# When the next weight unit is fetched in the attention layer, and where its subtraction stands in VectorE's order

## The chip, the cores and the metric

The kernel runs on one core of a Trainium2 chip. The metric is device time in microseconds (us) of one execution, as the median of several runs. A core has engines with instruction queues of their own: TensorE (PE, with its weight loads shown apart as PEld), VectorE (DVE), ScalarE (ACT), GpSimd (POOL) and SyncE (SP), which here only issues DMAs. Each engine works through its list in order; an instruction that has to wait holds what stands behind it in the same list.

## The reference

A trunk of four residual blocks on x of shape (1, 512, 1024) in float32: softmax attention, an MLP, a gated linear recurrence (RG-LRU), and again an MLP, with an RMSNorm ahead of each and one at the end. The change touches the attention alone:

```
qkv = einsum('bsd,de->bse', h, w_qkv).reshape(B, S, 3, 16, 64)
s = einsum('bqhd,bkhd->bhqk', q_c, k_band) * 64**-0.5 + bias    # relative bias, own chunk of 64 and 8 before
p = softmax(where(key_pos >= 0, s, -1e30))
o = einsum('bhqk,bkhd->bqhd', p, v_band);  out = o @ w_o        # out is added to the residual
```

## The kernel before

**Products.** A float32 product is made of three matmuls (`mm3`, lines 288 to 290): each operand is split into a rounded high part and the rest as a low part, and high by high, low by high and high by low are summed in one PSUM bank.

**Weight units.** The weights come as a list of units (`plan`), each a 128x1024 float32 tile of 512 KB. `fetch` (from line 140) takes the next unit: a DMA that SP issues (line 154) into one of three raw tiles `wr`, a cast on ACT that gives the high part `wh` (line 179), and a subtraction on DVE that gives the low part `wl` (line 184). `wh` and `wl` rotate through five buffers each. `prefetch(n)` fetches until n units are ready and not yet taken; `want(n)` prefetches n + `ahead` units and takes n. In the attention, `ahead` is 4, so a projection that begins on unit u fetches unit u+4 at its first line. In what follows wl18 is the subtraction of unit 18, and so on. Units 10 to 15 are the q and k projections of the head pairs 2 to 4 (q on the even number), 16 to 19 together the second half of the v projection (v1), 20 to 25 q and k of the pairs 5 to 7, 26 to 33 the output projection (wo), and then the MLP's.

**Attention.** 16 heads. For head h, `score` makes the scores on PE in three PSUM banks (lines 483 and 484); DVE adds the bias and takes the maximum while it reads them (line 487, tile `p`), negates it (491), ACT takes the exponential with a running sum (494), DVE makes the reciprocal (498) and scales (501, four instructions). `turn` transposes p on PE (line 514, ten matmuls into three banks `x`), ACT casts it (`pH`, 518) and DVE subtracts (`pL`, 519). `weigh` multiplies by v (529 and 530), and ACT and DVE bring the halves of a pair together (`ax` 535, `o` 536, `oH` 540, `oL` 541). Scores and transposes share one pool of four PSUM banks, taken in turn; projections have another four.

**Projections between the heads.** The projections of later pairs are a queue of small steps (`queue`, `fill`) put between the parts of the heads: q and k of a pair (`qk_steps`: 24 matmuls into one bank, then `q_out` or `k_out`), v (`v_steps`), and the output projection (`wo_steps`). `q_out` scales (tile `tq`, line 384), casts and subtracts (389). `k_out` scales (`tk`, line 394), casts each half on ACT (`kh`, 399), subtracts on DVE (`kl`, 400) and copies both to the other 64 partitions by 128 KB DMAs on SP (lines 401 and 402).

**Order.** The program is written in this order; a scheduler then sets the order on each engine by the order of the program and by its own estimate of when inputs are there, and may move instructions past each other. `tc.keep_in_program_order(ins)` keeps one instruction at its place in the program's order.

Of the kernel before, what the change touches and what calls it, by code (L numbers as in the profile page):

```python
# [35 lines left out]
def f(ap):  # L36
    return ap.bitcast(F32)
# [3 lines left out]
def trunk(ctx: ExitStack, tc: tile.TileContext, xT, cols, gfin, win, wqkv, wo, rwin, rga, rgx, rwo, w1, w2, out):  # L41
# [10 lines left out]
    def mmp(name):  # L52
        return ps.tile([P, T], F32, name=name, tag="mm")
# [46 lines left out]
    state = {"next": 0, "ready": [], "ahead": 4, "stop": None, "plain": 0}  # L100
    raws, start_, down, upper = {}, [], {}, {}

    def two(t):
        return t.rearrange("p (k c) -> p k c", k=2)
# [4 lines left out]
    def rows(src):  # L109
        return src.rearrange("(k p) c -> p k c", p=P)  # L110

    def load_down(key, name):
        if key not in down:
            return
        both = state["raw"].tile([P, 2, 1024], F32, name=f"b{name}_{key[0]}{key[1]}", tag=f"b{name}")
        for h in range(2):
            raws[name, h] = both[:, h]
            nc.sync.dma_start(two(raws[name, h]), rows(down[key][name][h * U : (h + 1) * U]))

    def first_sum(key):  # L120
        if key in down:
            for h in range(2):
                G.dma_start(raws["12", h], raws["11", h], accum_op=ALU.add)

    def load_up(key, name):
        if key not in upper:
            return
        if name in ("s1", "22"):
            raw = state["kept"][:, int(name == "22")]
        else:  # L130
            n = state["base"] + int(name == "12")
            raw = wraw.tile([P, 1024], F32, name=f"u{name}_{key[0]}{key[1]}", tag=f"wr{n % 3}")
        raws["u" + name] = raw
        nc.sync.dma_start(four(raw), rows(upper[key]["21" if name == "s1" else name]))
        if name == "s1":
            G.dma_start(four(raw), rows(upper[key]["22"]), accum_op=ALU.add)

    def fetch():
        i = state["next"]
# [4 lines left out]
        n, half = 1024, nk  # L144
        if kind[:5] == "plain":
            n = nk * sum(src.shape[1] for src in key)
# [37 lines left out]
        low = V.tensor_sub(L[:, :n], raw[:, :n], f(H[:, :n]))  # L184
        if not i:
            start_.append(low)
        if kind == "plain_":
            state["base"] = state["plain"] % 3
            load_up((nk_layer[i], 0), "11")
            load_up((nk_layer[i], 0), "12")  # L190
        elif kind == "us2" and key[1]:
            load_up(following, "s1")
        elif kind == "us3":
            load_up(following, "11")
        elif kind == "us4":
            load_up(following, "12")
        elif kind == "u22" and key[1]:
            load_up(following, "22")
        elif kind in ("11", "t1", "22", "21", "t2", "t3", "t4") and key[1] == 3:
            hs = slice(half * U, (half + 1) * U)  # L200
            if kind == "t1":
                nc.sync.dma_start(two(raws["11", half]), rows(down[key]["22"][hs]))
                G.dma_start(two(raws["11", half]), rows(down[key]["12"][hs]), accum_op=ALU.add)
            elif kind == "22":
                G.dma_start(raws["22", half], raws["12", half], accum_op=ALU.add)
        elif kind == "t2" and half:
            load_down(following, "12")
        elif kind == "t3" and half:
            load_down(following, "11")
        elif kind == "t4" and half:  # L210
            first_sum(following)
            load_down(following, "22")
            load_down(following, "21")
        state["ready"].append((nk, H[:, :n].rearrange("p (k c) -> p k c", k=nk), L[:, :n].rearrange("p (k c) -> p k c", k=nk)))

    def prefetch(n):
        while len(state["ready"]) < n and state["next"] < len(plan) and state["next"] != state["stop"]:
            fetch()

    def want(n):  # L220
        prefetch(n + state["ahead"])
        got = [state["ready"].pop(0) for _ in range(n)]
        nk = got[0][0]
        return (lambda k, c: got[k // nk][1][:, k % nk, c]), (lambda k, c: got[k // nk][2][:, k % nk, c])
# [62 lines left out]
    def mm3(acc, WH, WL, XH, XL, start, stop, more=False):  # L287
        PE.matmul(acc, WH, XH, start=start, stop=False, skip_group_check=more)  # L288
        PE.matmul(acc, WH, XL, start=False, stop=False, skip_group_check=more)  # L289
        PE.matmul(acc, WL, XH, start=False, stop=stop, skip_group_check=more)  # L290
# [75 lines left out]
    with ExitStack() as actx:  # L366
# [36 lines left out]
                kk[2 * p + hh] = (kh, kl)  # L403

        def qk_steps(p, out_):
            WH, WL = want(1)
            acc = mmp(f"qk{p}{out_.__name__}")
            c = slice(0, P)
            for k in range(KT):
                mm3(acc, WH(k, c), WL(k, c), hnH[k], hnL[k], k == 0, k == KT - 1)  # L410
                yield 2
            out_(p, acc)


        def v_steps(g):
# [20 lines left out]
        def wo_tile(m, acc, last):  # L436
            V.tensor_add(hT[m], acc, hT[m])
            if last:
                nm1.feed(m, False)

        def wo_steps(pairs, us, last):
            for u in us:
                WH, WL = want(1)
                for i in range(2):
                    acc = mmp(f"wo{pairs[0]}{2 * u + i}")
                    for n, p in enumerate(pairs):
                        mm3(acc, WH(n, PAIR[i]), WL(n, PAIR[i]), *oHL[p], n == 0, n == len(pairs) - 1)
                        yield 2
                    wo_tile(2 * u + i, acc, last)
# [99 lines left out]
        for k0, nk in FIRST:  # L549
            if k0 == 0:  # L550
                fetch()
                tc.keep_in_program_order(S.activation(spare, epsb, AF.Sqrt))
            for k in range(k0, k0 + nk):
                if k:
                    nc.sync.dma_start(hT[k], xT[k * P : (k + 1) * P, :])
                low = n0.split(k)
                if k < 2:
                    after(low, start_[k])
            if k0:
                fetch()  # L560
        for k in range(KT):
            n0.square(k)
        for k0, nk in FIRST:
            WH, WL = want(1)
# [17 lines left out]
        def qk(p):  # L582
            return [(f"q{p}", qk_steps(p, q_out), ("s", 2 * p - 3)), (f"k{p}", qk_steps(p, k_out), ("s", 2 * p - 3))]
# [4 lines left out]
        A, B = (0, 1, 2, 3), (4, 5, 6, 7)  # L588
        queue = vv_(0) + qk(2) + qk(3) + qk(4) + vv_(1) + qk(5) + qk(6) + qk(7)
        queue += [("woA", wo_steps(A, range(4), False), ("w", 7)), ("wo0", wo_open(B), ("w", 13))]  # L590
        queue += [("wo1", wo_close(B), ("w", 15)), ("woB", wo_steps(B, range(1, 4), True), ("w", 15))]
        at = {"s": -1, "w": -1}
        credit = [0]
# [501 lines left out]
    with ExitStack() as rctx:  # L1095
# [83 lines left out]
        for u in range(4):  # L1179
            WH, WL = want(2 if u > 1 else 1)  # L1180
# [21 lines left out]
        for u in range(4):  # L1202
            WH, WL = want(2)
# [34 lines left out]
        for u in range(2, 4):  # L1238
            WH, WL = want(2)
# [47 lines left out]
```

## Time and profile before

| | |
|---|---|
| median of 3 runs | 1032.16 us (1030.75 to 1032.8) |
| profiled execution | 1031.12 us |
| its span, first to last instruction | 1029.3 us |
| mean granted TensorE clock | 0.998 |
| PE busy, share of the span | 1017.8 us, 99% |
| DVE busy | 865.8 us, 84% |
| ACT busy | 665.8 us, 65% |

All positions below are microseconds from the start of the span. The attention with its projections runs from about 46 to 262. In a row of a timeline the first number is the start, the second the duration; consecutive instructions overlap a little, so that the distance of two starts is what one costs. "x3" joins three instructions of one kind that follow each other. In brackets stands the idle time before it and what ended it.

### The profile page before, as it was taken

The numbers are of one execution on the slowest core, as the hardware profiler recorded it, in microseconds if no ns is written. First come the engines' busy times: TensorE is split into PE (matmuls) and PEld (weight loads), VectorE is DVE, ScalarE is ACT, GpSimd is POOL, SyncE is SP. The second block draws the span as 40 slices with busy tenths as digits, with TensorE's granted clock in tenths as the row PEclk, the third lists the DMA queues.
The fourth block names the chain that finished last, engine by engine and source line by source line (L and its number), as shares of the span: only waits on it lengthen the run. The fifth ranks groups of instructions, "written<-read, shape, count | busy, mean of one in ns | idle before, by whom it ended". The sixth has DMA issues, their size and how long they took to land.

```text
span 1029.3 us, 15294 instructions
## 1 busy us (share of the span) xinstructions
PE 1017.8 (99%) x5762; PEld 892.2 (87%) x5762; DVE 865.8 (84%) x1222; ACT 665.8 (65%) x1020; POOL 100.1 (10%) x128
## 2 busy tenths in 40 slices
PE   9999999999999999999999999999999999999997
PEld 7888888888999999999988788888999999999986
DVE  7889788969789898698688989987789798698687
ACT  7566666646687566567567686645786566567565
POOL 1000001004111111111020000003111111111020
PEclk9999999999999999999999999999999999999999
DMA  8454254229929738828773412186838738728572
GB/s 268 126 142 122 83 156 119 74 78 249 246 51 236 206 63 209 221 49 215 203 144 94 135 62 67 58 256 176 223 60 227 205 60 215 217 48 218 143 162 85
DMA packets 125482, 153.62 MB, mean 149 GB/s; under 512 B 6497, under 2 KB 94561, under 8 KB 125409
## 3 DMA queue, kind: packets, MB, share of 16 engines
q1 hardware_dynamic: 102752, 114.18, 35.1%
q0 software_dynamic: 22080, 37.76, 21.1%
q8 instruction: 45, 0.74, 0.3%
q10 hardware_dynamic: 576, 0.72, 0.2%
q14 instruction: 29, 0.23, 0.1%
HBM read 123.27 MB, written 2.10 MB: 122 GB/s over the span
## 4 chain that ended last, share of the span: by engine, by line
PE 88%; DVE 7%; ACT 2%; DMA 1%; issue 1%; DVEq 0%; ACTq 0%; SPq 0%
PE m L290 9%; PE m L289 9%; PE m L288 9%; PE x L288 6%; PE x L289 6%; PE x L290 6%; PE y L288 4%; PE y L289 4%; PE y L290 4%; DVE wl L184 2%; PE v L288 1%; PE ro L290 1%; PE v L290 1%; PE yb L288 1%; PE yb L290 1%; PE v L289 1%
## 5 line engine op out<-in xcount | busy, mean ns | idle before, releaser
L184 DVE TENSOR_TENSOR wl<-b,wh 128x1024 fp32r<-128x1024 f32 x112 | 135.6, 1221 | 37.2 <-ACT wh L179 35.5
L179 ACT CAST wh<-b 128x1024 fp32r<-128x1024 f32 x112 | 116.7, 1051 | 61.5 <-PE m L289 19.1
L290 PE MATMUL m<-rH,wl 128*128 128x256 f32 x448 | 125.9, 281 | 0.0
L289 PE MATMUL m<-rL,wh 128*128 128x256 f32 x448 | 125.8, 281 | 0.0
L288 PE MATMUL m<-rH,wh 128*128 128x256 f32 x448 | 125.7, 281 | 0.0
L290 PE MATMUL m<-hnH,wl 128*128 128x256 f32 x336 | 95.0, 283 | 0.0
L289 PE MATMUL m<-hnL,wh 128*128 128x256 f32 x336 | 95.0, 283 | 0.0
L288 PE MATMUL m<-hnH,wh 128*128 128x256 f32 x336 | 94.9, 282 | 0.0
L179 ACT CAST wh<-wr 128x1024 fp32r<-128x1024 f32 (+1 forms) x65 | 66.9, 1030 | 42.2 <-PE ro L289 8.3
L289 PEld LDWEIGHTS m<-rL,wh 128*128 128x128 f32 x448 | 85.0, 190 | 1.2
L288 PEld LDWEIGHTS m<-rH,wh 128*128 128x128 f32 x448 | 84.8, 189 | 1.0
L184 DVE TENSOR_TENSOR wl<-wr,wh 128x1024 fp32r<-128x1024 f32 (+1 forms) x66 | 78.2, 1188 | 8.5 <-ACT wh L179 8.2
L290 PEld LDWEIGHTS m<-rH,wl 128*128 128x128 f32 x448 | 84.9, 189 | 0.0
L179 ACT CAST wh<-u 128x1024 fp32r<-128x1024 f32 x56 | 58.2, 1050 | 26.5 <-PE x L290 16.9
L184 DVE TENSOR_TENSOR wl<-u,wh 128x1024 fp32r<-128x1024 f32 x56 | 67.6, 1220 | 3.1 <-ACT wh L179 3.1
L289 PEld LDWEIGHTS m<-hnL,wh 128*128 128x128 f32 x336 | 64.3, 191 | 0.8
L288 PEld LDWEIGHTS m<-hnH,wh 128*128 128x128 f32 x336 | 64.2, 191 | 0.8
L290 PEld LDWEIGHTS m<-hnH,wl 128*128 128x128 f32 x336 | 64.3, 191 | 0.0
L288 PE MATMUL x<-wh,h 128*128 128x512 f32 (+1 forms) x132 | 50.9, 386 | 0.6 <-DVE d L1061 0.6
L290 PE MATMUL x<-wh,l 128*128 128x512 f32 (+1 forms) x132 | 50.9, 385 | 0.0
L289 PE MATMUL x<-wl,h 128*128 128x512 f32 (+1 forms) x132 | 50.7, 384 | 0.0
L288 PE MATMUL y<-wh,hs 128*128 128x512 f32 x128 | 50.2, 392 | 0.0
(384 smaller groups left out, 2890.2 us busy)
## 6 DMA issues: line engine op xcount, KB each, us to landing
b<-in_w SPq DMA_DIRECT2D x68, 512.0 KB, 5.8
b<-b POOLq DMA_DIRECT2D x36, 512.0 KB, 6.9
kept<-in_w SPq DMA_DIRECT2D x28, 512.0 KB, 4.3
u<-in_w SPq DMA_DIRECT2D x28, 512.0 KB, 6.2
wr<-in_wqkv SPq DMA_DIRECT2D x20, 512.0 KB, 4.6
wr<-in_rwin SPq DMA_DIRECT2D x16, 512.0 KB, 3.6
kept<-in_w POOLq DMA_DIRECT2D x14, 512.0 KB, 7.5
u<-in_w POOLq DMA_DIRECT2D x14, 512.0 KB, 7.4
```

What stands on the lines that cost most here:

```text
L179: high = S.copy(H[:, :n], raw[:, :n])
L184: low = V.tensor_sub(L[:, :n], raw[:, :n], f(H[:, :n]))
L288: PE.matmul(acc, WH, XH, start=start, stop=False, skip_group_check=more)
L289: PE.matmul(acc, WH, XL, start=False, stop=False, skip_group_check=more)
L290: PE.matmul(acc, WL, XH, start=False, stop=stop, skip_group_check=more)
```

## The change

In `qk_steps` and `wo_steps`, `want` takes its unit with 3 units ahead, where it was 4. The fourth is fetched later: in `qk_steps` once `out_` (that is `q_out` or `k_out`) has been written, and with the flag `behind`, by which the unit's subtraction keeps its place in the program's order; in `wo_steps` ahead of the second of its two output tiles, without the flag. `v_steps`, `wo_open`, the MLPs and the recurrence are as they were; v1's `want(4)` still fetches up to unit 23. The number of instructions and DMAs on each engine is the same; from the first MLP on the orders agree. Lines of the changed kernel are higher by 2 from line 187 on, and by 7 in the functions of the heads (the subtraction of pL is line 519 before, 526 after).

```diff
@@ -184,6 +184,8 @@
         low = V.tensor_sub(L[:, :n], raw[:, :n], f(H[:, :n]))
         if not i:
             start_.append(low)
+        if state.get("behind"):
+            tc.keep_in_program_order(low)
         if kind == "plain_":
             state["base"] = state["plain"] % 3
             load_up((nk_layer[i], 0), "11")
@@ -217,8 +219,8 @@
         while len(state["ready"]) < n and state["next"] < len(plan) and state["next"] != state["stop"]:
             fetch()
 
-    def want(n):
-        prefetch(n + state["ahead"])
+    def want(n, ahead=None):
+        prefetch(n + (state["ahead"] if ahead is None else ahead))
         got = [state["ready"].pop(0) for _ in range(n)]
         nk = got[0][0]
         return (lambda k, c: got[k // nk][1][:, k % nk, c]), (lambda k, c: got[k // nk][2][:, k % nk, c])
@@ -403,13 +405,16 @@
                 kk[2 * p + hh] = (kh, kl)
 
         def qk_steps(p, out_):
-            WH, WL = want(1)
+            WH, WL = want(1, 3)
             acc = mmp(f"qk{p}{out_.__name__}")
             c = slice(0, P)
             for k in range(KT):
                 mm3(acc, WH(k, c), WL(k, c), hnH[k], hnL[k], k == 0, k == KT - 1)
                 yield 2
             out_(p, acc)
+            state["behind"] = True
+            prefetch(4)
+            state["behind"] = False
 
 
         def v_steps(g):
@@ -440,8 +445,10 @@
 
         def wo_steps(pairs, us, last):
             for u in us:
-                WH, WL = want(1)
+                WH, WL = want(1, 3)
                 for i in range(2):
+                    if i:
+                        prefetch(4)
                     acc = mmp(f"wo{pairs[0]}{2 * u + i}")
                     for n, p in enumerate(pairs):
                         mm3(acc, WH(n, PAIR[i]), WL(n, PAIR[i]), *oHL[p], n == 0, n == len(pairs) - 1)
```

The following lists show the order at the places that matter. A row is line, operation, output<-inputs, size; the number behind a name tells tiles of one name apart and may differ by a few between the kernels.

VectorE at the end of the projection k3, before:

```order
L394 TENSOR_TENSOR tk3_946<-qk3k_out_870,n0acc_202 128x512
L491 TENSOR_SCALAR mx4_913<-mx4_913 128x4
L184 TENSOR_TENSOR wl18_1023<-wr18_1024,wh18_1022 128x1024
L519 TENSOR_TENSOR pL3_974<-x03_960,pH3_973 128x512
L519 TENSOR_TENSOR pL3_974<-x13_961,pH3_973 128x512
...
L400 TENSOR_TENSOR kl30_949<-tk3_946,kh30_948 64x512
L400 TENSOR_TENSOR kl31_955<-tk3_946,kh31_954 64x512
L519 TENSOR_TENSOR pL3_974<-x23_962,pH3_973 128x256
L536 TENSOR_TENSOR o1_990<-oa2_981,ax2_991 64x512
```

VectorE at the same place, now (above these rows, tk3, the negation of mx4 and pL3's first two subtractions follow each other with no weight subtraction between them):

```order
L402 TENSOR_TENSOR kl30_943<-tk3_940,kh30_942 64x512
L402 TENSOR_TENSOR kl31_949<-tk3_940,kh31_948 64x512
L184 TENSOR_TENSOR wl17_955<-wr17_956,wh17_954 128x1024
L526 TENSOR_TENSOR pL3_974<-x23_962,pH3_973 128x256
L543 TENSOR_TENSOR o1_990<-oa2_981,ax2_991 64x512
L494 ISA p5_997,mx5_998<-s25_996,bias1_896 128x512
```

The subtraction that stood between mx4 and pL3 is gone from there (it is unit 18's, which is now fetched after q4), and unit 17's now stands behind kl31, ahead of the last piece of pL3.

VectorE around the end of the projection k4, where v1 begins, before:

```order
L389 TENSOR_TENSOR q41_1079<-tq4_1074,q41_1079 64x512
L184 TENSOR_TENSOR wl19_1083<-wr19_1084,wh19_1082 128x1024
L536 TENSOR_TENSOR o1_990<-oa3_1092,ax3_1101 64x512
...
L491 TENSOR_SCALAR mx6_1124<-mx6_1124 128x4
L184 TENSOR_TENSOR wl20_1172<-wr20_1173,wh20_1171 128x1024
L400 TENSOR_TENSOR kl40_1160<-tk4_1157,kh40_1159 64x512
L498 RECIPROCAL sm6_1125<-sm6_1125 128x4
...
L501 TENSOR_SCALAR p6_1123<-p6_1123,sm6_1125 128x512
L400 TENSOR_TENSOR kl41_1166<-tk4_1157,kh41_1165 64x512
L519 TENSOR_TENSOR pL5_1215<-x05_1201,pH5_1214 128x512
```

And now:

```order
L498 TENSOR_SCALAR mx6_1118<-mx6_1118 128x4
L526 TENSOR_TENSOR pL5_1215<-x05_1201,pH5_1214 128x512
L526 TENSOR_TENSOR pL5_1215<-x15_1202,pH5_1214 128x512
L526 TENSOR_TENSOR pL5_1215<-x25_1203,pH5_1214 128x256
L505 RECIPROCAL sm6_1119<-sm6_1119 128x4
...
L508 TENSOR_SCALAR p6_1117<-p6_1117,sm6_1119 128x512
L402 TENSOR_TENSOR kl40_1154<-tk4_1151,kh40_1153 64x512
L402 TENSOR_TENSOR kl41_1160<-tk4_1151,kh41_1159 64x512
L184 TENSOR_TENSOR wl19_1166<-wr19_1167,wh19_1165 128x1024
L184 TENSOR_TENSOR wl20_1172<-wr20_1173,wh20_1171 128x1024
L543 TENSOR_TENSOR o2_1243<-oa4_1234,ax4_1244 64x512
L494 ISA p7_1259,mx7_1260<-s07_1256,bias1_896 128x128
```

Unit 19's subtraction stood behind q41, at the end of the projection before; now it stands behind both halves of kl4, with unit 20's right behind it. pL5 moved from behind kl41 to ahead of sm6.

On PE at this place, the eight score matmuls of head 7 stood behind the 21st of the 24 matmuls of v1's first bank, and now stand behind its 19th. The 20th is the first that reads wl19.

SyncE's DMAs around the end of k6, before:

```order
L154 DMA wr30_2055<-in_wo 128x4x256
L401 DMA kh60_1846<-kh60_1846 64x512
L401 DMA kh61_1852<-kh61_1852 64x512
L154 DMA wr31_2133<-in_wo 128x4x256
L402 DMA kl60_1847<-kl60_1847 64x512
L402 DMA kl61_1853<-kl61_1853 64x512
```

And now:

```order
L154 DMA wr29_2049<-in_wo 128x4x256
L403 DMA kh60_1840<-kh60_1840 64x512
L404 DMA kl60_1841<-kl60_1841 64x512
L403 DMA kh61_1846<-kh61_1846 64x512
L404 DMA kl61_1847<-kl61_1847 64x512
L154 DMA wr30_2085<-in_wo 128x4x256
```

The copies of kl60 and kl61 stood behind the load of unit 31; now they stand ahead of the load of unit 30.

TensorE around the first scores of the same pair (head 12; oa is head 10's weighted sum, qk7q and qk7k the projections of pair 7), before:

```order
L530 MATMUL oa_1935<-pH_1774,v_1195 128x128
L288 MATMUL qk7q_out<-hnH_83,wh_1509 128x512
...
L290 MATMUL qk7q_out<-hnH_83,wl_1510 128x512
L288 MATMUL qk7k_out<-hnH_76,wh_1595 128x512
...
L289 MATMUL qk7k_out<-hnL_85,wh_1595 128x512
L483 MATMUL s_1858<-kl_1847,q_1784 128x128
L484 MATMUL s_1858<-kh_1846,q_1784 128x128
```

And now:

```order
L536 MATMUL oa_1929<-pL_1769,v_1195 128x384
L490 MATMUL s_1858<-kl_1841,q_1778 128x128
L491 MATMUL s_1858<-kh_1840,q_1778 128x128
L490 MATMUL s_1858<-kl_1841,q_1778 128x256
...
L491 MATMUL s_1860<-kh_1840,q_1778 128x512
L521 MATMUL x_1896<-ident,p_1721 128x128 x4
...
L537 MATMUL oa_1929<-pH_1768,v_1195 128x384
```

The scores of head 12, which read kl60, stood behind five more matmuls of oa, three of qk7q and five of qk7k; now they stand ahead of them.

In the same part on VectorE, before head 13's scores are read (p13): before, pL11, q70, q71 and then p13 followed each other, with the reciprocal and the scaling of head 12 behind; now the reciprocal and the scaling of head 12 and o5 stand ahead of q70, and wl28 between q71 and p13. Before head 14's scores are read: before stood kl70, kl71, o5, two additions h0, oL5 and wl31; now kl70, kl71, wl29, o5, one addition h0, wl30 and oL5, with the other addition behind.

## The prediction

> **What bounds the kernel now.** The page's first part and the windows by stage come first. In the windows, the columns behind the stretch are its length and the busy time of PE, PEld, DVE, ACT and POOL, then the granted clock.
>
> ```profile
> PE 1017.8 (99%) x5762; PEld 892.2 (87%) x5762; DVE 865.8 (84%) x1222; ACT 665.8 (65%) x1020; POOL 100.1 (10%) x128
> ```
> ```profile
> 46.00:262.00 216.00, 213.23 (x1090) 180.88 (x1089) 181.24 (x411) 133.92 (x287) 19.54 (x35) 1.00 0.45 127
> ```
>
> TensorE is busy 99% of the span. In the attention, 46 to 262, which holds everything that the change moves, it is idle for 216.00 - 213.23 = 2.8 us. This is the most that an edit can win that adds and removes no matmul. DVE has 35 us of slack there on average, but it works through its list in order, so a subtraction in the wrong place can still make PE wait. Next the waits of PE, which name the idle time:
>
> ```profile
> PE s L483 <- DVE pL L519: 1.2, 1, 1.2
> PE s L483 <- DMA kl<-kl: 1.0, 1, 1.0
> PE x L514 <- DVE mx L487: 0.5, 1, 0.5
> ```
> ```profile
> L184 DVE TENSOR_TENSOR wl<-wr,wh 128x1024 fp32r<-128x1024 f32 x27 | 33.0, 1221 | 1.0 <-ACT wh L179 0.8
> ```
>
> The three lines are 2.7 of the 2.8 us. A weight subtraction costs 1.22 us, about 1.14 from start to start; 27 of them run here. The change moves subtractions and loads, so the question is which of the three stalls lose their cause, and where a moved subtraction makes a new one. I went through the places where one stands close to work that PE waits for.
>
> **A, around 87: a stall that loses its cause.**
>
> ```profile
> 85.18 1.06 ACT L518 CAST pH<-x 128x512 fp32r<-128x512 f32 x2
> 86.52 1.22 DVE L184 TENSOR_TENSOR wl<-wr,wh 128x1024 fp32r<-128x1024 f32 x1
> 87.65 1.28 DVE L519 TENSOR_TENSOR pL<-x,pH 128x512 fp32r<-128x512 f32 x2
> 88.39 0.44 PE L483 MATMUL s<-kl,q 128*128 128x384 f32 x1 [1.15 <-DVE pL L519]
> 195.61 0.34 PE L483 MATMUL s<-kl,q 128*128 128x384 f32 x1
> ```
>
> PE waits 1.15 us for head 3's pL, which reads out the bank that the next scores need. pL's first input was there by about 85.7 (a cast at 85.18, two in 1.06), yet DVE took wl18 first. Now no subtraction stands there, so pL begins at 86.52, 1.13 earlier. The restart goes too: the first matmul after the stall took 0.44 us, where the same shape without one took 0.34 (at 195.61). Sum -1.25; bounds 0 (PE's wait stays for another cause) and -1.25.
>
> **B, 172 to 178: a copy behind a weight load.**
>
> ```profile
> 170.96 1.26 ACT L399 CAST kh<-tk 64x512 fp32r<-64x512 f32 x2
> 172.57 1.40 DVE L400 TENSOR_TENSOR kl<-tk,kh 64x512 fp32r<-64x512 f32 x2
> 171.60 1.11 SPq L401 DMA_DIRECT2D kh<-kh  x2
> 172.81 0.55 SPq L154 DMA_DIRECT2D wr<-in_wo  x1
> 173.44 1.17 SPq L402 DMA_DIRECT2D kl<-kl  x2
> 176.18 0.39 PE L288 MATMUL qk7k_out<-hnH,wh 128*128 128x512 f32 x1
> 176.41 0.39 PE L289 MATMUL qk7k_out<-hnL,wh 128*128 128x512 f32 x1
> 177.81 0.30 PE L483 MATMUL s<-kl,q 128*128 128x128 f32 x1 [1.01 <-DMA kl<-kl]
> ```
> ```profile
> kh<-kh SPq DMA_DIRECT2D x2, 128.0 KB, 2.2
> kl<-kl SPq DMA_DIRECT2D x2, 128.0 KB, 4.2
> ```
>
> The copies of kh6 landed 2.2 us after issue; those of kl6, issued right behind the 512 KB of a weight unit, took 4.2, so the first was there at about 173.44 + 4.2 = 177.64. Head 12's scores were due at 176.41 + 0.23 = 176.64 and came at 177.81. Now the copies stand ahead of the load, and no weight subtraction stands ahead of kl60. But its reader moves up as well, past five matmuls of oa and eight of q and k. Eight at 0.23 (176.41 - 176.18) are 1.84; for the five, head 8's oa serves:
>
> ```profile
> 109.08 0.33 PE L530 MATMUL oa<-pH,v 128*128 128x384 f32 x1
> 109.66 0.45 PE L288 MATMUL v<-wh,hnH 128*128 128x512 f32 x1
> ```
>
> 0.58. So the scores are due at 176.64 - 2.42 = 174.22. kl60 needs kh60's cast (170.96 + 0.63 = 171.59), takes 0.70, is issued at about 172.3 and lands 2.2 later, at 174.5: 0.3 us late instead of 1.01. I take -0.7; bounds -1.1 (on time, and no restart) and 0 (a load still in flight ahead of the copy). The Trainium skill, "DMA: Bandwidth & Descriptors", section "Anatomy of one DMA — SWDGE (gpsimd) path", fits a transfer as 2.0 us and its bytes at 436 GB/s, for GpSimd's path. That is an estimate of 2.3 us for 128 KB, which the 2.2 bears out, and of 3.5 us if the copy has the load's 512 KB ahead of it, where the trace has 4.2. By the page the load explains a stall of only 0.3 us, nothing is won at B, and the whole sum is +0.7 higher; the measured 4.2 decides.
>
> **C, around 111: v1's fourth unit becomes late.** Before, wl19 was done at 102.
>
> ```profile
> 100.78 1.22 DVE L184 TENSOR_TENSOR wl<-wr,wh 128x1024 fp32r<-128x1024 f32 x1
> 108.58 0.18 DVE L498 RECIPROCAL sm<-sm 128x4 f32<-128x4 f32 x1 [1.08 <-ACT p L494]
> 108.79 1.28 DVE L501 TENSOR_SCALAR p<-p,sm 128x128 f32<-128x128 f32 x4
> 110.10 0.69 DVE L400 TENSOR_TENSOR kl<-tk,kh 64x512 fp32r<-64x512 f32 x1
> 110.63 0.39 PE L289 MATMUL v<-wl,hnH 128*128 128x512 f32 x1
> 111.76 0.22 PE L483 MATMUL s<-kl,q 128*128 128x128 f32 x1
> 113.04 0.40 PE L288 MATMUL v<-wh,hnH 128*128 128x512 f32 x1
> ```
>
> Now it stands behind head 6's reciprocal, its four scalings and both halves of kl4. The reciprocal waits 1.08 us for ACT's exponentials, so nothing ahead of it makes it later, except that ACT now casts pH5 first, which I count as 0.15. Then 108.73 + 1.4 (scalings) + 1.4 (two kl) + 1.22 puts the end of wl19 at 112.75, less some 0.4 by which the heads' work runs ahead after A: 112.35. Its first reader ran at 110.63; head 7's scores now stand ahead of it (113.04 - 111.76 = 1.28), which makes 111.91. PE arrives earlier by what A gives and D takes, 0.85: 111.06. The wait is 1.3 by this; the lead of 0.4 could be anything up to the 1.13 of A, so I take a little less, +1.1. Bounds: +0.2 (PE no earlier, the chain 0.25 quicker) and +2.2 (pH5's casts, 1.35 us as a group, push the exponentials fully).
>
> **D, around 93: wl17 ahead of pL3's last piece.**
>
> ```profile
> 91.13 1.40 DVE L400 TENSOR_TENSOR kl<-tk,kh 64x512 fp32r<-64x512 f32 x2
> 92.56 0.42 DVE L519 TENSOR_TENSOR pL<-x,pH 128x256 fp32r<-128x256 f32 x1
> 93.44 1.25 PE L514 MATMUL x<-ident,p 128*128 128x128 f32 x10
> ```
>
> pL3's last piece ended at 92.98 and frees the bank of head 4's last two transposes, which ran near 94.2 (ten in 1.0 us from 93.44). With wl17 in front it ends at 92.98 + 1.14 - 0.43 (DVE's lead after A) = 93.7, and PE is there 1.15 earlier, at 93.05: up to 0.65 late. Since the reciprocal between them hangs on ACT, I take +0.4; bounds 0 and +1.14, the whole subtraction.
>
> **E and F, heads 13 and 14.**
>
> ```profile
> 182.13 1.39 DVE L389 TENSOR_TENSOR q<-tq,q 64x512 fp32r<-64x512 f32 x2
> 183.55 0.29 DVE L487 CUSTOM_DVE_ANT_0 p<-s,bias 128x128 f32<-128x128 f32 x1
> 185.22 1.26 PE L514 MATMUL x<-ident,p 128*128 128x128 f32 x10
> 193.21 0.69 DVE L536 TENSOR_TENSOR o<-oa,ax 64x512 f32<-64x512 f32 x1
> 195.74 1.22 DVE L184 TENSOR_TENSOR wl<-wr,wh 128x1024 fp32r<-128x1024 f32 x1
> 197.57 0.92 PE L514 MATMUL x<-ident,p 128*128 128x128 f32 x6 [0.55 <-DVE mx L487]
> ```
>
> E: before, DVE read head 13's first scores right behind q7; their bank is the one that head 12's transposes take from 185.22 on. Now wl28 and head 12's scaling stand in front, while the scores of head 12 come 2.4 us earlier and pull that scaling with them. The two nearly cancel; +0.3, bounds 0 and +1.14. F: the read of head 14's scores came behind wl31 and cost PE 0.55 us at 197.57. Now wl29 and wl30 stand between kl7 and it, and one addition (0.6, half of a pair) behind: 1.14 - 0.6 = +0.5 on a chain that was already late. PE's stall at E gives part back: +0.3; bounds -0.55 and +0.6. Its scores also come two matmuls earlier (0.46) than the 0.3 us by which kl70's copy was early: +0.2, bounds 0 and +0.5.
>
> Elsewhere a unit that is fetched at the end of a projection still has three other units ahead of it, each with 24 matmuls of 0.23 (5.5 us), before its first matmul; and from the first MLP on the order is the old one.
>
> **Sum.** -1.25 - 0.7 + 1.1 + 0.4 + 0.3 + 0.3 + 0.2 = +0.35 us. The profiled execution took 1031.12 (span 1029.3 and 1.82 around it), which gives 1031.47; it lies 1.04 below the median of 1032.16, so on the scale of the median I say **1032.5 us**. By the bounds alone the sum runs from -2.9 (A and B gone, F's stall gone, +0.2 at C) to +5.6 (nothing won, everything at its upper end).
>
> **Rivals.** *Faster:* the subtractions held back hide, as DVE has 16% free; C, D and E cost nothing, and A, B and the 0.55 at F go: -1.25 - 0.7 - 0.55 = -2.5, 1029.7. For it speaks that all three stalls have their cause in a weight unit fetched too soon; against it that C's chain hangs on ACT and comes out late by over 1 us. *Slower:* the held subtraction itself is the new bound. VectorE's list is in order, so each puts 1.14 us between a projection's result and the head whose scores or transposes hold the PSUM banks; with C at 2.2, D and E at 1.14, F at 1.1 against A and B: 5.6 - 1.95 = +3.6, 1035.8. It decides once wl19 ends after about 113 and the read of head 13's scores begins after about 185. For it speaks that A is this same mechanism in the kernel before; against it the 35 us of free DVE time, and that PE's next steps do not all need the banks. *Not what it says:* the copies' readers move up as far as the copies do, or another load lies ahead of them, and B's stall stays: +0.35 + 0.7 = +1.05, 1033.2.
>
> **Chances.** The forecast 0.57, the faster rival 0.10, the slower 0.21, the copy that stays late 0.12. A measurement here tells about 0.2%, 2.06 us, from no change. The faster rival passes that mark narrowly (0.08 of its 0.10), the slower one mostly (0.19 of 0.21), the others hardly (0.01): faster 0.08, same 0.72, slower 0.20. The forecast's own range is 1031 to 1034; to hold 8 in 10 it reaches half into each outer case, 1030.3 to 1034.9.
>
> **What would show it.** Right: in the waits of PE the line for pL is gone and the one for kl at most 0.4; a new line "v, waiting for wl" of about 1 us near 111; short waits of transposes near 93 and 184 to 198; a granted clock of 1.00; the same busy time of every engine. A is wrong if pL still waits behind something at 87; B if kl60's copy takes much over 2.3 us; C if wl19 ends before 111. The forecast as a whole is wrong if PE's idle time in the attention is under 1.5 us or over 5.

## The result, and the profile after

The changed kernel takes 1033.44 us (median of 21 runs, 1032.69 to 1036.78), the kernel before 1031.6 us (21 runs, 1030.75 to 1032.8). The ratio is 1.0018, with a 95% interval of 1.0012 to 1.0024: slower by 1.84 us. This is a hair inside the 0.2% that the prediction called no change, but it is clear of zero. The prediction said 1032.5 and no measurable change; its first median, 1032.16, came from three of these runs.

The page's first part and the waits of TensorE, of the changed kernel:

```profile
PE 1019.6 (99%) x5762; PEld 892.3 (86%) x5762; DVE 866.5 (84%) x1222; ACT 665.3 (64%) x1020; POOL 100.7 (10%) x128
```
```profile
PE x L521 <- DVE mx L494: 1.3, 2, 0.8
PE v L291 <- DVE wl L184: 1.3, 1, 1.3
PE y L291 <- DVE wl L184: 0.5, 1, 0.5
PE s L490 <- DVE pL L526: 0.3, 1, 0.3
PE x L521 <- DVE pL L526: 0.3, 1, 0.3
```

The wait for pL fell from 1.2 to 0.3 (place A), the one for the copy of kl is gone (B). In their stead PE waits 1.3 us for the weight subtraction wl19 in v1 (C), 0.3 for pL's last piece (D), and 1.3 in two parts for DVE's read of scores: 0.8 at E, which is new, and 0.5 at F, which stood there before (0.55). 0.5 stand in the first MLP, where nothing was expected. In the attention, 46 to 262, PE is idle for 216.00 - 212.77 = 3.2 us, where it was 2.8.

A row's idle time leaves out that a matmul after a wait also runs longer and that the one before it is still counted as busy. The starts of the same matmul in both kernels give the whole. The four that follow stand behind the transposes of the heads 2, 5, 8 and 15 and have the same number of matmuls ahead of them (350, 509, 686 and 1094) in every kernel whose stretches are told here. TensorE's timeline before, and then after:

```profile
74.77 0.48 PE L288 MATMUL qk3q_out<-hnH,wh 128*128 128x512 f32 x1
105.62 0.48 PE L288 MATMUL v<-wh,hnH 128*128 128x512 f32 x1
139.14 0.48 PE L288 MATMUL qk5q_out<-hnH,wh 128*128 128x512 f32 x1
219.32 0.48 PE L288 MATMUL wo<-oH,wh 128*128 128x512 f32 x1
```
```profile
74.53 0.48 PE L290 MATMUL qk3q_out<-hnH,wh 128*128 128x512 f32 x1
105.52 0.48 PE L290 MATMUL v<-wh,hnH 128*128 128x512 f32 x1
140.63 0.48 PE L290 MATMUL qk5q_out<-hnH,wh 128*128 128x512 f32 x1
221.08 0.48 PE L290 MATMUL wo<-oH,wh 128*128 128x512 f32 x1
```

So the stretch with A and D takes 30.85 us before and 30.99 after; the one with C 33.52 and 35.11; the one with B, E and F 80.18 and 80.45; from there to the end of the span 809.98 and 810.92. The change loses 1.6 us at C, and at D, E and F it gives back what A and B bring. Behind the attention another 0.9 go, of which the wait in the first MLP is 0.47.

**Place by place, after.** The rows are of the timelines of DVE, PE, ACT and SP of the changed kernel. A and D:

```profile
86.86 1.28 DVE L526 TENSOR_TENSOR pL<-x,pH 128x512 fp32r<-128x512 f32 x2
87.59 0.44 PE L490 MATMUL s<-kl,q 128*128 128x384 f32 x1 [0.31 <-DVE pL L526]
88.19 0.50 PE L490 MATMUL s<-kl,q 128*128 128x512 f32 x1
92.47 1.23 DVE L184 TENSOR_TENSOR wl<-wr,wh 128x1024 fp32r<-128x1024 f32 x1
93.61 0.42 DVE L526 TENSOR_TENSOR pL<-x,pH 128x256 fp32r<-128x256 f32 x1
94.18 0.41 PE L521 MATMUL x<-ident,p 128*128 128x128 f32 x2 [0.27 <-DVE pL L526]
```

pL now follows the negation of mx4 directly. The third pair of scores waits 0.31 us for its first piece instead of 1.15, and the fourth, which now stands right behind, starts 0.60 us later with a matmul of 0.50, as after a wait, just when the second piece of pL ends (86.86 + 1.28 = 88.14). The transposes ahead of these scores slip too: from their first to the next product PE takes 85.31 - 84.02 = 1.29 us, where it took 85.26 - 84.25 = 1.01, and DVE reads head 4's scores, which share that pool of banks, 0.34 us later (83.94 and 83.60). The list of waits shows 0.02 of this. At D the last piece of pL waits behind wl17, as the list says, and the last two transposes come 0.27 us late. By the starts D costs 0.47: from the first transpose to the next product PE takes 94.34 - 92.87 = 1.47 us, where it took 94.44 - 93.44 = 1.00. The same subtraction reaches further than the prediction followed it. DVE and ACT before, and then after:

```profile
94.22 0.17 DVE L491 TENSOR_SCALAR mx<-mx 128x4 f32<-128x4 f32 x1
95.17 0.40 ACT L494 ACTIVATE p<-p,mx 128x128 f32<-128x128 f32 x1
97.50 0.18 DVE L498 RECIPROCAL sm<-sm 128x4 f32<-128x4 f32 x1 [0.69 <-ACT p L494]
```
```profile
95.75 0.15 DVE L498 TENSOR_SCALAR mx<-mx 128x4 f32<-128x4 f32 x1
95.78 1.05 ACT L179 CAST wh<-wr 128x1024 fp32r<-128x1024 f32 x1 [0.79 <-PE qk4q_out L291]
96.73 0.40 ACT L501 ACTIVATE p<-p,mx 128x128 f32<-128x128 f32 x1
99.06 0.18 DVE L505 RECIPROCAL sm<-sm 128x4 f32<-128x4 f32 x1 [1.63 <-ACT p L501]
```

Head 5's maximum is negated 1.5 us later: wl17 and one of head 4's pL now stand ahead of it. It is there at 95.90, but ACT is not free. The cast of a weight unit, by its order unit 19's, now stands ahead of head 5's exponentials and waits for q4's last matmul; before, it stood behind them, at 98.91. So the exponentials begin at 96.73 and not at 95.17, the reciprocal of head 5 comes 1.56 later, and TensorE is at the same place as before (105.62 and 105.52). Of these 1.56 us, 0.80 are left at head 6's reciprocal (108.58 before, 109.38 after). C:

```profile
109.38 0.18 DVE L505 RECIPROCAL sm<-sm 128x4 f32<-128x4 f32 x1 [0.84 <-ACT p L501]
110.78 1.40 DVE L402 TENSOR_TENSOR kl<-tk,kh 64x512 fp32r<-64x512 f32 x2
112.22 2.36 DVE L184 TENSOR_TENSOR wl<-wr,wh 128x1024 fp32r<-128x1024 f32 x2
111.83 0.40 PE L290 MATMUL v<-wh,hnH 128*128 128x512 f32 x1
113.50 0.50 PE L291 MATMUL v<-wl,hnH 128*128 128x512 f32 x1 [1.27 <-DVE wl L184]
```

wl19 is the first half of the pair at 112.22 and ends at about 113.4. PE was ready for it at 111.83 + 0.23 = 112.06 and started at 113.50, 1.44 us later. B:

```profile
173.66 0.47 SPq L404 DMA_DIRECT2D kl<-kl  x1
kl<-kl SPq DMA_DIRECT2D x2, 128.0 KB, 2.3
176.03 0.30 PE L490 MATMUL s<-kl,q 128*128 128x128 f32 x1
```

The copies land in 2.3 us, kl60's at about 173.66 + 2.3 = 175.96, and the scores begin at 176.03 with no idle time put down. By the starts 0.18 us are left, as the matmul ahead began at 175.68 and one of its size takes 0.17. E:

```profile
185.43 1.23 DVE L184 TENSOR_TENSOR wl<-wr,wh 128x1024 fp32r<-128x1024 f32 x1
186.57 0.28 DVE L494 CUSTOM_DVE_ANT_0 p<-s,bias 128x128 f32<-128x128 f32 x1
187.27 0.92 PE L521 MATMUL x<-ident,p 128*128 128x128 f32 x6 [0.79 <-DVE mx L494]
```

Between q7 (until 185.4) and the read of head 13's scores stands wl28, and head 12's transposes stop for 0.79 us until the bank is read.

### The profile page after: what moved, and what is told of

Read it like the earlier page. It is cut to its first block, busy times and chain, and to the rows that moved or that the text cites. A ratio compares the mean times of both kernels' runs of the same rounds, so it can differ in the third digit from the quotient of the medians.

```text
span 1032.0 us, 15284 instructions
## 1 busy us (share of the span) xinstructions
PE 1019.6 (99%) x5762; PEld 892.3 (86%) x5762; DVE 866.5 (84%) x1222; ACT 665.3 (64%) x1020; POOL 100.7 (10%) x128
## 4 chain that ended last, share of the span: by engine, by line
PE 91%; DVE 4%; ACT 2%; issue 1%; DMA 1%; DVEq 0%; SPq 0%; POOL 0%; ACTq 0%; POOLq 0%
PE m L292 9%; PE m L291 9%; PE m L290 9%; PE x L290 5%; PE x L291 5%; PE x L292 5%; PE y L291 4%; PE y L290 4%; PE y L292 4%; PE x L521 1%; PE ro L292 1%; PE yb L292 1%; PE yb L290 1%; PE ro L290 1%; PE yb L291 1%; PE u L291 1%
## 5 line engine op out<-in xcount | busy, mean ns | idle before, releaser
L291 PE MATMUL y<-wl,hs 128*128 128x512 f32 x128 | 50.1, 391 | 0.5 <-DVE wl L184 0.5
```

## The experiments

Each kernel was timed over five rounds beside the kernel before, and differences are to its median in the same rounds. The table at the end of this section has the stretches between the marker matmuls for all of them.

### Without the flag

```diff
-        if state.get("behind"):
-            tc.keep_in_program_order(low)
```

> The change without the flag that holds the subtraction in its place; the later fetch stays. Theory 1 (the held place of the subtraction is what acts: the scheduler, left free, puts it back where it stood): the waits of the kernel before return, 1.0 to 1.2 us of the scores for pL near 88 and about 1 us for the copy of kl near 177; no wait of v for wl near 111, none of transposes for pL near 93; time within 0.7 us of the kernel before (ratio 0.9994 to 1.0006). Theory 2 (the fetch itself, 3 units ahead in place of 4, brings units late): the wait of v for wl stays over 1 us and the time stays 1.3 to 2.3 us above the kernel before.

Measured 1032.43 against 1031.52, ratio 1.0009 (1.0000 to 1.0017). Waits of TensorE in it:

```profile
PE s L488 <- DMA kl<-kl: 0.9, 1, 0.9
PE s L488 <- DVE pL L524: 0.8, 1, 0.8
PE y L289 <- DVE wl L184: 0.8, 1, 0.8
PE x L519 <- DVE mx L492: 1.5, 2, 1.0
```

The waits of the kernel before are back (0.8 for pL, 0.9 for kl) and the wait for wl19 at C is gone, so theory 2 falls: the later fetch by itself does not bring units late. TensorE's list is the same as before, and DVE's differs in a few rows. The time is 0.9 us above the kernel before and not within 0.7: a new stop of transposes of 1.0 us near 85, where o0 and oL0 have changed places with reads of scores, and 0.8 in the MLP.

### The q and k projections alone

```diff
-                WH, WL = want(1, 3)
+                WH, WL = want(1)
                 for i in range(2):
-                    if i:
-                        prefetch(4)
```

> The change in the q and k projections alone; the output projection fetches as before. Theory 1: nothing in the attention's waits differs from the changed kernel (pL 0.3, wl 1.3 near 111, transposes 0.3 near 93 and 0.8 near 186 and 0.5 near 199), since the output projection's part moves only the units at the attention's end; the 0.5 us wait of the MLP's y for wl near 296 goes if that part causes it, and the time is then 1.2 to 1.8 us above the kernel before, otherwise 1.6 to 2.2. Rival (the output projection's later fetch is where the loss comes from): time within 0.7 us of the kernel before.

Measured 1033.05 against 1031.52, ratio 1.0015 (1.0006 to 1.0023). The waits in the attention are those of the changed kernel to 0.1 us, with 1.3 at C; none stands in the MLP. So the loss comes from the q and k projections, and the output projection's part is worth the 0.3 us between the two differences (1.84 and 1.53), which these intervals do not tell from nothing.

### Unit 19 fetched as before

```diff
-            WH, WL = want(1, 3)
+            WH, WL = want(1, 4 if p == 4 and out_ is k_out else 3)
```

> The changed kernel with one unit fetched as before: k4 takes its unit with 4 ahead, so that unit 19, the fourth of v1, is fetched ahead of k4 and not behind it. Theory 1 (wl19 held behind kl4 is the largest new wait): the 1.3 us wait of v near 111 goes, at the price of at most 0.5 us for head 5's transposes near 104; the other waits stay; time 0.8 to 1.4 us below the changed kernel, 0.4 to 1.0 above the kernel before. Rival (the wait only moves on, to the next reader of DVE's queue): a wait of 1 us or more near 104 to 115, time as the changed kernel, 1.4 to 2.3 above the kernel before.

Measured 1032.29 against 1031.52, ratio 1.0009 (1.0000 to 1.0018).

```profile
PE x L521 <- DVE mx L494: 2.1, 3, 0.8
```

The wait of v for wl is gone from the list, 1.1 us come back of the changed kernel's 1.84, and the wait for mx counts three times where it counted two: the new one, 0.7 us near 105, is larger than the 0.5 that was allowed, since wl18 and wl19 together now stand ahead of the read of head 6's scores. Theory 1 holds in its sign and its place, and half of the rival's too: part of the stall only moved on.

### k4 alone

```diff
-            WH, WL = want(1, 3)
+            late = f"{out_.__name__[0]}{p}" in ('k4', '')
+            WH, WL = want(1, 3 if late else 4)
...
+            if late:
                 state["behind"] = True
                 prefetch(4)
                 state["behind"] = False
```

The output projection is as before here and in the kernels that follow.

> The kernel before with the later fetch and the held subtraction for k4 alone, which puts wl19 behind kl41. Theory 1 (C by itself, as the fourth unit of v1 has no projection between its fetch and its first reader): a wait of v for wl of 0.4 to 1.3 us near 111, smaller than in the changed kernel as PE comes there later by A's wait; the waits of the kernel before stay; time 0.4 to 1.4 us above the kernel before. Rival (C needs the rest of the change, head 7's scores drawn ahead and A's lead): a wait under 0.2 us and a time within 0.3 us of the kernel before.

Measured 1032.55 against 1031.79, ratio 1.0008 (0.9999 to 1.0017).

```profile
PE v L291 <- DVE wl L184: 0.5, 1, 0.5
```

C stands by itself, 0.5 us in the list of waits and 34.45 - 33.52 = 0.93 from marker to marker, and the waits at A (1.4) and B (1.0) are still there. In the changed kernel it is 1.6. There wl19 begins 112.22 - 105.52 = 6.70 us behind the marker at 105, here 110.46 - 106.08 = 4.38, as ACT begins head 6's exponentials 1.53 us behind the marker there (107.05) and 0.77 ahead of it here (105.31). Of these 2.3 us, 1.3 are covered there by head 7's scores, which in the changed kernel stand ahead of wl19's first reader and here behind it.

### q4 alone, q7 alone, and both

The diff is that of k4 alone, with ('q4', ''), ('q7', '') or ('q4', 'q7').

> The kernel before with the later fetch and the held subtraction for q4 alone, which takes wl18 out of the place between mx4 and pL3. Theory 1 (A by itself): the wait for pL near 87 falls from 1.15 to about 0.3, the waits for kl near 177 (1.0) and at 197 (0.55) stay, no new wait over 0.3; time 0.4 to 1.0 us below the kernel before. Rival (what A wins returns at B or behind it, where PE waits for a copy that hangs on DVE): the kl wait grows by what A loses and the time is within 0.3 us of the kernel before.

Measured 1030.68 against 1031.79, ratio 0.9993 (0.9984 to 1.0002).

```profile
PE s L490 <- DVE wl L184: 1.3, 1, 1.3
PE s L490 <- DVE pL L526: 0.3, 1, 0.3
```

The wait for pL is 0.3; the one at B is 1.3 (its row is put down to wl, but it stands at the first scores of head 12, at the same place). The stretch of A takes 30.71, where the four traces with wl18 in its old place and PE's list unchanged there (before, before again, k4 alone, q7 alone) take 30.85, 31.37, 31.57 and 31.57. So A brings 0.6 us against their mean of 31.34, half of what the prediction took. The last three differ from the first in the time of four instructions on DVE (see "The kernel before, profiled again"); this run is like them, and against their mean of 31.50 A brings 0.8.

> The kernel before with the later fetch and the held subtraction for q7 alone, which puts the copies of kl6 ahead of the load of unit 31. Theory 1 (B is won and paid back at E): the kl wait near 177 falls from 1.0 to under 0.3, the pL wait near 88 stays at 1.15, a wait of 0.8 to 1.1 us for head 12's transposes appears near 186, the one at 197 shrinks to about 0.3; time from 0.6 below to 0.3 above the kernel before. Rival (B's win is kept): no wait over 0.4 us near 186 and a time 0.8 to 1.3 us below.

Measured 1031.53 against 1031.79, ratio 0.9998 (0.9989 to 1.0007).

The wait for kl is no longer listed, and one of 1.0 us for the read of head 13's scores has come up near 187, with two weight subtractions (2.36 us) between q7 and that read. The wait for pL is 1.5, not 1.15. The stretch with B, E and F takes 80.07, against 80.18 and 80.39 in the two traces of the kernel before. B is won and paid back at E, as theory 1 has it.

> The kernel before, with the later fetch and the held subtraction for the projections q4 and q7 alone (units 18 and 29 to 31, those at the stalls A and B). Theory 1 (each stall has its own subtraction or load as its cause): the pL wait near 88 and the kl wait near 177 go, 0.8 to 1.2 us each; no wait near 93 and 111; one near 184 of up to 0.9 us for head 12's transposes; together 1.0 to 2.2 us below the kernel before. Rival (the stalls move on to the next place and what is won is given back): within 0.6 us of the kernel before.

Measured 1030.59 against 1031.52, ratio 0.9992 (0.9984 to 1.0001): 0.9 us faster by the medians, just short of the 1.0 of theory 1; the interval just reaches 1. The waits listed in the attention are A's rest, 0.3, and E, 1.0.

The expectation named units 29 to 31 for q7; the subtraction held there is unit 28's, and the load that leaves the copies' way is unit 31's.

### The subtraction at E held later

Against the run with q4 and q7: unit 28 is fetched behind the fourth step of k7, and in a second kernel at the end of k7, behind kl71.

```diff
-            late = f"{out_.__name__[0]}{p}" in ('q4', 'q7')
+            late = f"{out_.__name__[0]}{p}" in ('q4',)
-            WH, WL = want(1, 3 if late else 4)
+            WH, WL = want(1, 3 if late or p == 7 and out_ is q_out else 2 if p == 7 else 4)
...
                 mm3(acc, WH(k, c), WL(k, c), hnH[k], hnL[k], k == 0, k == KT - 1)
+                if p == 7 and out_ is k_out and k == 3:
+                    state["behind"] = True
+                    prefetch(3)
+                    state["behind"] = False
```

> The kernel of the run with q4 and q7 alone, but unit 28 is fetched, and its subtraction held, behind the fourth of the eight steps of k7 instead of right behind q7, so that the read of head 13's scores stands ahead of it. Theory 1 (the 1.0 us wait near 185 is the held subtraction standing ahead of that read): that wait goes; the copies of kl7 now follow the held subtraction, so up to 0.7 us may appear for kl near 193; time 0.3 to 1.0 us below the run with q4 and q7. Rival (the bank is late because head 12's scaling moved ahead of the read, not because of wl28): a wait of 0.8 us or more stays near 185, and the time is within 0.3 us of that run.

> As the run that held unit 28 behind the fourth step of k7, but held behind kl71, at the end of k7. Theory 1 (a held subtraction costs what it stands directly ahead of): the 0.7 us wait for kl7's copies near 194 falls under 0.3; the read of head 14's scores now has units 28 to 30 ahead of it, so the wait of the transposes near 197 grows to 0.4 to 0.8; time 1.0 to 1.8 us below the kernel before. Rival (kl7's copies are late for another reason): the wait for kl stays at 0.6 or more.

Measured 1030.44 against 1031.79, ratio 0.9990 (0.9981 to 0.9999), and 1030.5 against 1031.7, ratio 0.9987 (0.9978 to 0.9996). Waits, behind the fourth step and then behind kl71:

```profile
PE s L494 <- DMA kl<-kl: 0.7, 1, 0.7
PE x L525 <- DVE mx L498: 0.2, 1, 0.2
```
```profile
PE s L490 <- DMA kl<-kl: 0.4, 1, 0.4
PE x L521 <- DVE mx L494: 0.7, 2, 0.5
```

The wait near 185 is gone in both, so E was the held subtraction ahead of the read, and not head 12's scaling, which stands ahead of it still. Where the subtraction goes to, something else becomes late: kl7's copies by 0.7 with wl28 ahead of them, by 0.4 with it behind; and in the second the read of head 14's scores by 0.5 again. The kl wait at the end of k7 did not fall under 0.3 as expected. The stretch with B, E and F takes 79.84 and 79.86, 0.4 less than before. Both are faster than the kernel before, by 1.35 and 1.2 us of the medians, with intervals clear of 1.

### The copies of kl on another queue

```diff
-                nc.sync.dma_start(f(kl[oth]), f(kl[own]))
+                nc.gpsimd.dma_start(f(kl[oth]), f(kl[own]))
```

> The kernel before with the copies of kl issued by GpSimd instead of SyncE, all else in place; so at B the copy of kl60 no longer stands behind the weight load in one queue, but the load still moves its 512 KB at the same time. Theory 1 (the load's bytes on the shared DMA engines make the copy late): it lands over 3.2 us after issue while the load runs, the wait near 177 stays at 0.6 us or more, time from 0.3 below to 1.0 above the kernel before. Rival (the place in the one queue is what counts): it lands in 2.2 to 2.9 us, the wait near 177 is under 0.3, time 0.3 to 1.0 us below.

Measured 1037.4 against 1031.7, ratio 1.0051 (1.0037 to 1.0065).

```profile
PE s L483 <- DMA kl<-kl: 5.1, 3, 2.2
kl<-kl POOLq DMA_DIRECT2D x2, 128.0 KB, 3.5
```
```profile
kl<-kl POOLq DMA_DIRECT2D x2, 128.0 KB, 2.3
kl<-kl POOLq DMA_DIRECT2D x2, 128.0 KB, 4.1
```

Beside the weight load the copies of kl6 take 3.5 us from the other queue too (issued 1.0 us behind it), where the ones of kh, issued ahead of the load, take 2.2. The last two of these rows are those of kl3, with no load in flight, and of kl5, issued 0.65 us behind a load (windows 92 to 95.5 and 153 to 158): 2.3 and 4.1, as much as the 4.2 in one queue. So it is the load that is in flight which makes the copy late, and not the place in one queue. The loss of 5.7 us was foreseen by neither theory: the waits for kl come at three places, 5.1 us in all, one of them at the scores behind kl5's copies, which stood ahead of the load in the kernel before; and the scheduler had put the scores of some heads elsewhere in TensorE's list.

### The kernel before, profiled again

> The kernel before, unchanged, a second look at its trace. The waits that differ between the runs without following an edit (0.2 to 0.35 us of transposes near 84, 1.3 or 1.6 for pL near 87, 0 to 1.4 for the MLP's y near 294): if they are the spread from one execution to the next, this trace differs from the first in them by as much; if they come from the edits, it shows none near 84, 1.15 near 87 and none near 294, as the first.

One run of 1031.23 us.

A is 1.45 here and was 1.15; B is 1.25 (with its row put down to wl) and was 1.01; no stop is listed near 84, none in the MLP. For A the traces show what differs. The first two rows are the four scalings of head 3's softmax and GpSimd's four copies of the bias in the first trace, the next two the same in this one:

```profile
76.88 1.27 DVE L501 TENSOR_SCALAR p<-p,sm 128x128 f32<-128x128 f32 x4
77.83 1.60 POOL L377 COPY bias<-bias 128x256 f32<-128x256 f32 x4 [52.40 <-DMA bias<-in_win]
```
```profile
76.57 1.61 DVE L501 TENSOR_SCALAR p<-p,sm 128x128 f32<-128x128 f32 x4
77.03 1.75 POOL L377 COPY bias<-bias 128x256 f32<-128x256 f32 x4 [52.34 <-DMA bias<-in_win]
```

The copies begin when a DMA has landed, 0.95 us behind the scalings' start in the first trace and 0.46 in this one, and the scalings take 0.34 longer where more of them run beside the copies. All thirteen traces fall into these two groups: 1.26 or 1.27 us where the copies begin 0.95 or later (before, changed, q and k alone, unit 19 as before), 1.55 to 1.61 where they begin within 0.5 (the other nine). The waits for pL of 1.4 and more, and the listed stops of 0.1 to 0.2 near 84, stand in the second group alone. So the wait at A varies by 0.3 us between executions of one kernel, and the trace on which the prediction rests was of the group with the shorter one, as is that of the changed kernel. What makes B's wait vary, and the one in the MLP near 294, stays open.

### The stretches of all kernels

From marker to marker on TensorE, us, and from the last marker to the end of the span:

| kernel | 74 to 105 (A, D) | to 139 (C) | to 219 (B, E, F) | to the end | median less that of before |
|---|---|---|---|---|---|
| before | 30.85 | 33.52 | 80.18 | 809.98 | |
| before, again | 31.37 | 33.52 | 80.39 | 809.81 | |
| changed | 30.99 | 35.11 | 80.45 | 810.92 | +1.84 |
| without the flag | 31.75 | 33.52 | 80.07 | 810.81 | +0.91 |
| q and k alone | 30.80 | 35.08 | 80.50 | 809.84 | +1.53 |
| unit 19 as before | 31.77 | 33.54 | 80.43 | 809.79 | +0.77 |
| k4 alone | 31.57 | 34.45 | 80.21 | 810.16 | +0.76 |
| q4 alone | 30.71 | 33.53 | 80.45 | 809.78 | -1.11 |
| q7 alone | 31.57 | 33.52 | 80.07 | 809.77 | -0.26 |
| q4 and q7 | 30.57 | 33.53 | 80.04 | 810.72 | -0.93 |
| held in k7's fourth step | 30.69 | 33.53 | 79.84 | 812.17 | -1.35 |
| held behind kl71 | 30.74 | 33.53 | 79.86 | 810.72 | -1.20 |
| kl on another queue | 31.41 | 33.53 | 85.61 | 810.31 | +5.70 |

Each stretch is of one profiled execution, the last column of all timed runs. The C stretch agrees to 0.02 us wherever C's order is the old one; the last stretch is 809.8 to 810.3 where the MLP has little or no wait for wl near 294, and 810.7 to 812.2 in the five kernels where that wait is 0.5 or more. The first stretch of "unit 19 as before" holds the new stop near 105.

## Why the prediction was right, and where its sum was off

The time fell into the range, 1030.3 to 1034.9, and into the outcome that had 0.72, by 0.2 us. The mechanism was the forecast's: two stalls lose their cause, and held subtractions make new ones at the places that it named. Its size was not: the sum said +0.35 on the scale of the first median of 1032.16, where 21 runs of the kernel before give 1031.6, so the change itself is 1.5 us worse than the sum. That the forecast of 1032.5 lies within 1 us of the result is partly luck, as that first median was 0.56 too high; so is the outcome, with 0.2 us to spare. Of the signs, the wait of v for wl (1.3 us near 113), the short waits of transposes, the clock of 1.00 and PE's idle time of 3.2 us came; the line for pL did not go but fell to 0.3.

By the stretches the attention loses 0.14 + 1.59 + 0.27 = 2.0 us against the first trace of the kernel before, which is of the same group of scalings. By its terms:

- **A, -1.25: -0.6.** Right in the mechanism (q4 alone takes most of the wait away), off in its size. The step that failed is "pL begins at 86.52, 1.13 earlier": it began at 86.86, as DVE came 0.34 later to the reads of head 4's scores. Of the idle time 0.84 went and 0.3 stayed, and 0.24 came back at the fourth pair of scores, which waits for pL's second piece. The later reads also cost 0.3 at the transposes near 84, which the sum does not have.
- **B, -0.7: -1.0.** The slip of 177.81 - 176.64 = 1.17 us fell to 0.18; the bounds held it. That the load explained the 4.2 us is supported by the copies on the other queue, 3.5 and 4.1 behind a load and 2.3 without one. The prediction's estimate from the fit in the Trainium skill, "DMA: Bandwidth & Descriptors", section "Anatomy of one DMA — SWDGE (gpsimd) path", was 3.5 us for a copy with the load's bytes ahead of it, and so nothing to win at B; the trace had 4.2, and the stop did go.
- **C, +1.1: +1.6.** The right place and sign. Measured 1.44 in PE's starts and 1.6 in the stretch, inside the bounds of 0.2 to 2.2. The chain was as drawn (reciprocal, four scalings, two kl, wl19), but it began at 109.38 and not at 108.73. The failed step is "less some 0.4 by which the heads' work runs ahead after A". wl17, costed at D for the bank alone, also stood ahead of head 5's maximum, and unit 19's cast on ACT stood ahead of its exponentials. The cast ended last; the two made head 5's softmax 1.56 us late and head 6's 0.80, instead of 0.4 early. No run separates them.
- **D, +0.4: +0.5.** Measured 0.27 of idle time, 0.47 with the starts.
- **E, +0.3: +1.0.** Measured 0.79 of idle time, about 0.95 with the starts; inside the bounds. "The two nearly cancel" is the step that failed: the scaling did move up with the scores, but wl28 still stood ahead of the read, and with the subtraction held later the wait is gone.
- **F, +0.3 and +0.2: about +0.2.** The wait is 0.52 against 0.55 before, and the one for kl7's copies did not come in this kernel; 0.2 is what B and E leave of the stretch's 0.27.
- **The rest, 0.** The 0.5 us in the first MLP was not seen. It is in five of the thirteen traces, and no edit explains which.

The rivals: the faster one is out, and the copy did not stay late. The slower one's two signs both came, as wl19 ended at about 113.4 and head 13's scores were read from 186.57 on. So the held subtraction was the bound where it said, with too large a price: C 1.6, D 0.5 and E 0.95 against 2.2, 1.14 and 1.14, none of them reached. (The terms named for the lower bound, A, B, F and C, add up to -2.7 and not to -2.9.) The change's own idea was half right: of the twelve q and k projections that it touches, q4 alone brings 1.1 us by the medians and k4 alone costs 0.8 (both intervals reach 1).

## What to carry to other kernels

On an engine that works in order, a cheap instruction with slack has a price that is set by what stands directly behind it: 1.2 us of weight subtraction cost nothing in most places, and 0.5 to 1.6 us of TensorE where it stood ahead of the read that frees a PSUM bank, or where its own reader came next. So hold it at the places where the trace shows a stall with that cause, and leave the rest to the scheduler; the same rule put on every projection gave back more than it won. And when several such moves are summed, walk the list of each engine from the first of them on, the one that casts as well as the one that subtracts: an instruction that is costed where it first makes another engine wait also delays what comes after.

## What the runs showed that was not expected

A 128 KB copy within SBUF takes 2.2 us alone and 4.2 right behind a 512 KB load on the same queue, and 3.5 to 4.1 when another queue issues it behind such a load: moving it to another queue does not protect it, issuing it first does. Matmuls that restart after a wait ran 0.1 us longer (0.44 and 0.50 us where 0.34 and 0.39 are usual), and the granted clock was 1.00 in the two microseconds with the stop at C (the changed kernel's windows: length, busy times of the five engines, clock):

```profile
112.00:114.00 2.00, 0.73 (x3) 0.47 (x3) 1.97 (x3) 0.00 (x0) 0.00 (x0) 1.00 0.70 161
```

Four scalings on DVE took 1.27 us alone and 1.55 to 1.61 where GpSimd's copies of the bias ran beside more of them, and one wait of TensorE differed by 0.3 us between two executions of one kernel with it. That is as much as several terms of the sum.
